# Windowed attention of a hybrid layer: one plan over 64 head groups in pinned order, 129-column value products, gates projected last

## The chip, the cores and the metric

The kernel runs on one core of one Trainium2 chip. The metric is the device time of one execution in microseconds (us); less is better. The engines of the core are named PE (TensorE: matmuls and transposes; PEld is its weight load), DVE (VectorE), ACT (ScalarE), POOL (GpSimd) and SP (SyncE, which here only issues DMAs). Each takes its own instructions in order and waits at semaphores for the others.

## The reference, cut to what matters

A latent stream x of 2048 tokens by 1024 and 256 context tokens go through two layers and a last norm. The even layer mixes by a Fourier transform and by latent attention (8 heads); the odd layer is the one that changes. Its last part per block of 128 tokens is:

```python
h = rmsnorm(x, norm_g[1]) * (1 + scale) + shift
q, k, v, g = split(h @ o_w_in, (1024, 256, 256, 1024))      # rotary on q and k; k, v for the context too
for kv in range(4):                                         # 4 heads of 64 share one k and v
    s = q[block, 4 * kv : 4 * kv + 4] @ k[context + own and both neighbouring blocks].T / 8   # |i - j| <= 128
    m = max(s, sink);  p = exp(s - m)
    o[block, kv] = p @ v / (p.sum() + exp(sink - m))
x = rmsnorm(x + gate * ((o * silu(g)) @ o_w_out), final_g)
```

All of it is float32. The kernel makes float32 products from 2 or 3 matmuls of rounded halves: a value is split into a high part (a cast) and a low part (value minus cast).

## The kernel before, in words

The odd layer starts with its projection. The 18 pieces of 128 tokens (2 of them context) are worked in three sets, and each set goes through five column blocks, one pass each: 0 and 1 are q, 2 is k and v, 3 and 4 are gates. `TP['p2o']` is the order of the columns in the last set; in the other sets it is 0 to 4. So before the change the last five passes are gate, gate, q, q, k with v. Passes write q, k, v (high and low parts) and silu(g) to DRAM (`store_t`, `g1d`), from where the attention loads them. `e6` is a list of work for the attention that is done between the matmuls of the last four passes: constants, keys and values of the first tiles (`prep_k`), q of block 0 (`load_q6`), row maxima of block 0 (`max_all`: four `max_band` and two `max_ctx` for a head group), its `chain`, and the first `aug`.

The attention runs over 16 blocks of 128 tokens, in each over 4 key-value heads, in each over 5 key tiles of 128 (2 of context, 3 of the band; 4 in blocks 0 and 15). One head group is one (block, kv) with its 4 heads: 64 of them, 312 steps (`step6`). A step makes scores for 128 keys by 4 heads x 128 queries in one PSUM bank: a bfloat16 mask matmul (L1813, outer tiles only), L1814 and L1815. The rows appended to the second operand (`Q2`, rows 64 and up) carry the negative maximum, split in halves and picked by a mask: `aug` transposes it (L1566) and multiplies it into place (L1567). ACT then takes the exponential twice, into float32 `pf` (L1819) and float16 `ph` (L1820), and POOL, for some steps DVE, makes the low part `pl` (L1821). The products with v are queued (`pvq`) and done 4 steps later (`lag`): for each of 4 heads L1831 (high by high with the column of ones: 65 columns), L1832 (high by low, 64 columns, into the same 64 columns) and L1833 (low by high, 65). After the last tile of a group DVE makes the quotient (L1837, L1838, L1840) and POOL multiplies it into the gates (L1842).

The maxima of block b + 1 are made during block b: PE makes the scores once more (L1525 for the band, L1538 for the context), DVE reduces them (L1529, L1541), and at 0.94 of the block one `chain` of six DVE operations (L1549 to L1556), one addition and one exponential (L1562) serves all 16 heads. Also in block b + 1 the output of block b is finished: two `out_tr` (4 transposes each, L1868, and a split), 16 `out_mm` of 3 matmuls (`mm3`, L186 to L188), then `out_fin` (square, power, the scaling L1894, the store).

All this stands in one `plan` per block: `at(place, function)` with the place as a share of the block's steps; after each step the plan's functions that are due are called. PE's, DVE's, ACT's and POOL's instructions go to a scheduler, which may change their order; SP's DMAs keep the order in which they are called. The weights of the output projection are loaded and split (`wload`, `wsplit`) in blocks 0 and 1.

## Time and profile before

| | |
|---|---|
| median of 3 runs | 3035.95 us (3033.46 to 3040.3) |
| profiled execution | 3034.24 us, its span 3032.2 us, mean granted TensorE clock 0.983 |
| busy share of the span | PE 94%, POOL 54%, DVE 48%, ACT 47% |
| first score of blocks 0, 1, 2, 14, 15 | 2335.02, 2377.05, 2420.61, 2935.42, 2976.23 us |

The span is the time from the first to the last instruction that the profiler saw; the execution is some 2 us longer. A row of the windows gives a stretch and its length, the busy time of each engine with the number of its instructions in brackets, the mean granted clock of TensorE as a share of full speed (PEclk), the busy share of the DMA engines and GB/s. A row of a timeline gives start and length of an instruction, its engine and line, what it writes and reads, how many of the same kind follow each other (x), and in square brackets how long the engine stood idle before it and what ended that. PE's matmuls are pipelined: rows of neighbours overlap, and the distance of two starts is what one costs. A row of the waits says which line waited for which. A group of instructions has busy us and the mean ns of one, then idle time before it and what ended most of that.

### The profile page before, as it was taken

The numbers are of one execution on the slowest core, as the hardware profiler recorded it, in microseconds if no ns is written. First come the engines' busy times: TensorE is split into PE (matmuls) and PEld (weight loads), VectorE is DVE, ScalarE is ACT, GpSimd is POOL, SyncE is SP. The second block draws the span as 40 slices with busy tenths as digits, with TensorE's granted clock in tenths as the row PEclk, the third lists the DMA queues.
The fourth block names the chain that finished last, engine by engine and source line by source line (L and its number), as shares of the span: only waits on it lengthen the run. The fifth ranks groups of instructions, "written<-read, shape, count | busy, mean of one in ns | idle before, by whom it ended". The sixth has DMA issues, their size and how long they took to land. (4 is left out here: it accounts for less than half of the span.)

```text
span 3032.2 us, 54284 instructions
## 1 busy us (share of the span) xinstructions
PE 2861.0 (94%) x21388; PEld 2299.7 (76%) x21388; DVE 1462.6 (48%) x2884; ACT 1427.4 (47%) x2131; POOL 1632.0 (54%) x1221
## 2 busy tenths in 40 slices
PE   7999999999999999999999998999997899999998
PEld 4787777877777777777777888989786666677666
DVE  3323315453656665666542234323234666676664
ACT  4333213223577777777773332232222645554554
POOL 2202204035588888888784434353443766766665
PEclk9999999999999999999999998999998999999999
DMA  6453335466310111011016545544464333223321
GB/s 240 153 177 134 130 122 173 142 213 223 104 44 26 44 40 44 26 44 40 26 35 232 188 153 177 187 141 162 152 189 156 105 105 98 84 77 93 102 83 45
DMA packets 299399, 357.13 MB, mean 118 GB/s; under 512 B 40884, under 2 KB 210172, under 8 KB 299144
## 3 DMA queue, kind: packets, MB, share of 16 engines
q1 hardware_dynamic: 231320, 258.73, 27.0%
q10 hardware_dynamic: 67824, 94.93, 8.9%
q8 instruction: 168, 2.75, 0.4%
q14 instruction: 87, 0.71, 0.1%
HBM read 245.82 MB, written 107.76 MB: 117 GB/s over the span
## 5 line engine op out<-in xcount | busy, mean ns | idle before, releaser
L186 PE MATMUL psb<-sbr 128*128 128x512 f32 (+3 forms) x2054 | 744.3, 363 | 14.4 <-ACT sbf L1022 5.7
L188 PE MATMUL psb<-sbr 128*128 128x512 f32 (+3 forms) x2054 | 722.9, 352 | 4.8 <-DVE sbr L183 4.8
L187 PE MATMUL psb<-sbr 128*128 128x512 f32 (+3 forms) x2054 | 723.8, 352 | 2.2 <-POOL sbr L183 2.2
L1188 POOL TENSOR_TENSOR sbf<-sbf 128x1024 f16<-128x1024 f32 (+1 forms) x296 | 624.2, 2112 | 140.8 <-ACT sbf L1187 76.9
L155 PE MATMUL psb<-sbr 100*128 100x512 f32 (+1 forms) x2408 | 624.2, 399 | 21.0 <-DVE sbr L955 14.4
L155 PEld LDWEIGHTS psb<-sbr 100*128 100x128 f32 (+1 forms) x2408 | 425.0, 190 | 112.8 <-issue 17.3
L942 DVE TENSOR_REDUCE sbf<-psb 128x1 f32<-128x512 f32 (+1 forms) x584 | 400.7, 690 | 218.1 <-PE psb L155 203.5
L186 PEld LDWEIGHTS psb<-sbr 128*128 128x128 f32 (+1 forms) x2054 | 390.7, 190 | 81.0 <-issue 12.3
L188 PEld LDWEIGHTS psb<-sbr 128*128 128x128 f32 (+1 forms) x2054 | 390.2, 190 | 63.9 <-DVE sbr L183 6.8
L187 PEld LDWEIGHTS psb<-sbr 128*128 128x128 f32 (+1 forms) x2054 | 390.8, 190 | 53.2 <-POOL sbr L183 3.9
L1821 POOL TENSOR_TENSOR sbf<-sbf 128x512 f16<-128x512 f32 x282 | 338.0, 1213 | 116.0 <-issue 60.1
L1186 ACT ACTIVATE sbf<-psb 128x1024 f32<-128x1024 f32 (+1 forms) x296 | 299.6, 1012 | 200.4 <-PE psb L155 180.5
L183 DVE TENSOR_TENSOR sbr<-sbf,sbr 128x512 fp32r<-128x512 f32 (+3 forms) x212 | 209.1, 1014 | 382.2 <-ACT sbr L180 381.1
L180 ACT CAST sbr<-sbf 128x512 fp32r<-128x512 f32 (+4 forms) x286 | 198.2, 731 | 394.5 <-PE psb L187 149.5
L183 POOL TENSOR_TENSOR sbr<-sbf,sbr 128x512 fp32r<-128x512 f32 (+4 forms) x113 | 166.1, 1482 | 367.9 <-ACT sbr L180 226.3
L1819 ACT ACTIVATE sbf<-psb 128x512 f32<-128x512 f32 x312 | 188.4, 604 | 282.1 <-PE psb L1815 249.8
L1187 ACT ACTIVATE sbf<-psb 128x1024 f16<-128x1024 f32 (+1 forms) x296 | 297.8, 1006 | 0.0
L155 PEld LDWEIGHTS <-sbf 128*128 128x128 f16 x4672 | 213.5, 97 | 72.9 <-issue 65.9
L155 PE MATMUL psb<-sbf 128*128 128x129 f16 (+1 forms) x4672 | 256.8, 207 | 5.2 <-DVE sbf L1214 2.9
L1529 DVE CUSTOM_DVE_ANT_0 sbf<-psb,sbf 128x384 bf16<-128x384 f32 (+1 forms) x256 | 137.8, 538 | 119.4 <-PE psb L1525 108.1
L1820 ACT ACTIVATE sbf<-psb 128x512 f16<-128x512 f32 x312 | 188.2, 603 | 5.5 <-DMA vd<-sbf 5.5
L1831 PEld LDWEIGHTS <-sbf 128*128 128x128 f16 x1248 | 115.5, 97 | 68.3 <-issue 61.8
(259 smaller groups left out, 4303.9 us busy)
## 6 DMA issues: line engine op xcount, KB each, us to landing
sbf<-in_o_w_in_t SPq DMA_DIRECT2D x60, 512.0 KB
sbf<-in_w_in_t SPq DMA_DIRECT2D x54, 512.0 KB
sbf<-in_x SPq DMA_DIRECT2D x32, 512.0 KB
sbf<-in_w_mod SPq DMA_DIRECT2D x32, 512.0 KB
sbr<-q1h SPq DMA_DIRECT2D x128, 128.0 KB
h1d<-sbf ACTq DMA_DIRECT2D x9, 1024.0 KB
sbf<-h1d SPq DMA_DIRECT2D x18, 512.0 KB
x1d<-sbf ACTq DMA_DIRECT2D x16, 512.0 KB
```

What stands on the lines that cost most here:

```text
L155: tc.keep_in_program_order(nc.tensor.matmul(*args, **kw))
L180: act.copy(hi, src)
L183: e_lo.tensor_sub(lo, src, hi)
L186: pe.matmul(ps, sh, mh, start=start, stop=False)
L187: pe.matmul(ps, sh, ml, start=False, stop=False)
L188: pe.matmul(ps, sl, mh, start=False, stop=stop)
L942: dve.reduce_max(st["mx"][:, js[0] : js[-1] + 1, c], ps[:, 0 : len(js) * kn].rearrange("p (j k) -> p j k", k=kn), axis=AX.X)
L1186: act.activation(pf[:, :, 0:n], ps[:, :, 0:n], AF.Exp, scale=MLA_SCALE)
L1187: act.activation(ph[:, :, 0:n], ps[:, :, 0:n], AF.Exp, scale=MLA_SCALE)
L1188: pool.tensor_sub(pl[:, :, 0:n], pf[:, :, 0:n], ph[:, :, 0:n])
L1819: act.activation(pf, ps, AF.Exp, scale=GQA_SCALE)
L1821: (dve if (TP["b0"].get("sub", TP["sub"]) if b == 0 else TP["sub"])[kv][n] else pool).tensor_sub(pl, pf, ph)
```

## The change

The order of columns in the last projection set becomes 0, 1, 2, 3, 4. `e6` holds the maxima, chain and aug of two head groups of block 0 where it held all four. The stores of gates wait one turn (`pend`) behind the other work of their pass.

In the attention, PE's instructions are no longer the scheduler's: `pe = pe_ordered` keeps them in the order of the calls. The 16 plans become one, in steps over all 312: for a group that starts at step s, q is asked for at the start of the group five before, the maxima at s - 9 to s - 4.9, the chain at s - 4.9, aug at s - 2.2. The chain is now per group: one DVE reduction over band, context and sink, one ACT copy that scales by -1, one POOL addition, one ACT exponential. The appended rows are 4 instead of 8. `out_tr` and `out_mm` come later in the next block (8.2, 10.2 and from 12.2 steps on, each 0.95 step), so that half of them reach into the block after; block 14 and the end are tighter.

Steps go in pairs. The float32, high and low tiles of a pair are one tile each, POOL subtracts both steps at once (128x1024), and value products are done two steps at a time, at least 6 steps late. A value product is now 129 columns (high by high with the ones, and high by low beside it) and 65 columns (low by high); their order alternates so that a burst ends with 129. The output of a group therefore takes two PSUM banks, and there is one such tile where there were two of one bank; DVE adds the second half with four operations per group. The final scaling of a block goes from DVE to an ACT copy, a POOL product and an ACT product.

The diff, cut to its core:

```diff
-    'p2o': [3, 4, 0, 1, 2],
+    'p2o': [0, 1, 2, 3, 4],
...
+    def chain(b, kv):
+        m = sm6.tile([P, 4], F32, tag="m", name=f"m6_{b}_{kv}")
+        dve.reduce_max(m, C6["mx", 4 * (b % 2) + kv], axis=AX.X)
+        v = VM[b, kv] = sm6.tile([P, 4], F32, tag="vm", name=f"vm6_{b}_{kv}", bufs=3)
+        act.activation(v.bitcast(F32R), m, AF.Copy, bias=SHIFT / GQA_SCALE, scale=-1.0)
+        es = ES[b, kv] = sm6.tile([P, 4], F32, tag="es", name=f"es6_{b}_{kv}", bufs=4)
+        pool.tensor_add(es, v, C6["sk8"][:, 4 * kv : 4 * kv + 4])
+
+    def sink(b, kv):
+        act.activation(ES[b, kv], ES[b, kv], AF.Exp, scale=GQA_SCALE)
...
     def aug(b, kv):
...
+        pe.transpose(ps[0:4, 0:P], VM[b, kv], ident)
...
+            Q2[b, kv][64:68, :].rearrange("p (j t) -> p j t", t=P),
+            ps[0:4, None, 0:P].to_broadcast([4, 4, P]), C6["mask4"],
...
     e6 = [
...
+        [const6, nop, *pk[0], nop, *pk[1], nop, *pk[2], nop, *pk[3]],
+        [nop] * 4 + [lambda: load_q6(0, 0)] + [nop] * 4,
+        [nop] * 4 + max_all(0) + [lambda: chain(0, 0)],
+        [lambda: load_q6(0, 1), lambda: load_q6(0, 2), *pk[4]] + [nop] * 4 + max_all(1) + [lambda: chain(0, 1), nop]
+        + [lambda: aug(0, 0)],
     ]
...
+    pe = pe_ordered
+    pps, ppv, ppo = psum(3), psum(1), psum(1)
...
+    def step6(b, kv, n, t, nk, x):
...
+        if not x:
+            PF["f"] = pp6.tile([P, 2, 512], F32, tag="pf", name=f"pf6_{b}_{kv}_{t}", bufs=2)
+            PF["h"] = pp6.tile([P, 2, 512], F16, tag="ph", name=f"ph6_{b}_{kv}_{t}")
+            PF["l"] = pp6.tile([P, 2, 512], F16, tag="pl", name=f"pl6_{b}_{kv}_{t}")
+        pf, ph, pl = PF["f"], PF["h"][:, x], PF["l"][:, x]
+        act.activation(pf[:, x], ps, AF.Exp, scale=GQA_SCALE)
         act.activation(ph, ps, AF.Exp, scale=GQA_SCALE)
...
+        if b == 15 and kv == 3 and n > 1:
+            (pool if x else dve).tensor_sub(pl, pf[:, x], ph)
+        elif x:
+            pool.tensor_sub(PF["l"], pf, PF["h"])
...
         def pv():
...
+                O[b, kv] = ppv.tile([P, 1024], F32, tag="o", name=f"o6_{b}_{kv}")
...
+                o = O[b, kv][:, j * 256 : j * 256 + 129]
...
+                if j % 2 and n:
+                    pe.matmul(o[:, 0:65], pl[:, js], v[:, kv, 0:65], start=False, stop=False)
+                    pe.matmul(o, ph[:, js], v[:, kv, 0:129], start=False, stop=last)
+                else:
+                    pe.matmul(o, ph[:, js], v[:, kv, 0:129], start=n == 0 and j % 2 == 0, stop=False)
+                    pe.matmul(o[:, 0:65], pl[:, js], v[:, kv, 0:65], start=False, stop=last and j % 2 == 1)
...
+                dve.tensor_add(den, p4[:, :, 64:65], ES[b, kv][:, :, None])
...
                 dve.tensor_mul(t1, p4[:, :, 0:64], den.to_broadcast([P, 4, 64]))
+                for j in range(4):
+                    dve.scalar_tensor_tensor(t1[:, j], p4[:, j, 65:129], den[:, j], t1[:, j], op0=ALU.mult, op1=ALU.add)
...
+                pool.tensor_mul(g, g, t1)
+        pvq.append((pv, n == nk - 1))
...
         v = sm6.tile([P, 1], F32, tag="v", name=f"v6s_{b}")
         y = sm6.tile([P, 1], F32, tag="y", name=f"y6s_{b}")
-        dve.tensor_scalar(v, ss, 1.0 / D, EPS, op0=ALU.mult, op1=ALU.add)
+        act.activation(v, ss, AF.Copy, bias=EPS, scale=1.0 / D)
         rsqrt(y, v)
-        dve.scalar_tensor_tensor(x, x, y, C6["fgb"], op0=ALU.mult, op1=ALU.mult)
+        pool.tensor_mul(x, x, C6["fgb"])
+        act.mul(x, x, y)
         sp.dma_start(out[b * P : (b + 1) * P, :], x)
...
+    nts = [len(tiles_of(b)) for b in range(16)]
+    S = [4 * sum(nts[:b]) for b in range(17)]
+    groups = [(b, kv) for b in range(16) for kv in range(4)]
+    start = [S[b] + kv * nts[b] for b, kv in groups]
+    plan = []
...
+    at(-1, lambda: (sink(0, 0), sink(0, 1)))
+    for u, (b, kv) in enumerate(groups):
+        if u > 2:
+            at(start[u - 5] + 0.3 if u > 5 else -1, lambda b=b, kv=kv: load_q6(b, kv))
+        if u > 1:
+            s0 = start[u] - 9
+            for j in range(4):
+                at(s0 + 0.8 * j, lambda b=b, kv=kv, j=j: max_band(b, kv, j))
+            for jj in range(2):
+                at(s0 + 3.2 + 0.8 * jj, lambda b=b, kv=kv, jj=jj: max_ctx(b, kv, jj))
+            at(s0 + 4.1, lambda b=b, kv=kv: (chain(b, kv), sink(b, kv)))
+        if u:
+            at(start[u] - 2.2, lambda b=b, kv=kv: aug(b, kv))
+    for x in range(TP["wa"], 17):
+        w0 = 1.5 * (x - TP["wa"] - 1) if x > TP["wa"] else -1
+        if x < 16:
+            at(w0, lambda x=x: wload(*wl_[x]))
+        if x > TP["wa"]:
+            at(w0 + 1.6, lambda x=x: wsplit(*wl_[x - 1]))
+    at(S[1] + 1, out_const)
+    for b in range(16):
+        at(S[b] - 0.5, lambda b=b: g_load(b))
+        if b < 13:
+            at(S[b] + 6.6, lambda b=b: [f() for f in prep_k(b + 5)])
         if b == 15:
+            break
+        s1 = S[b + 1]
+        t0, t1, m0, md = (8.2, 10.2, 12.2, 0.95) if b < 13 else (8.2, 10.2, 12.2, 0.45) if b == 13 else (3, 6, 6.5, 0.42)
+        at(s1 + t0, lambda b=b: out_tr(b, 0))
+        at(s1 + t1, lambda b=b: out_tr(b, 1))
+        at(s1 + m0, lambda b=b: out_load(b))
+        for i in range(16):
+            at(s1 + m0 + md * i, lambda b=b, i=i: out_mm(b, i // 8, i % 8))
+        at(s1 + m0 + md * 16 + 0.6, lambda b=b: out_fin(b))
+    at(S[15] + 14, lambda: out_load(15))
+    at(S[15] + 13.4, lambda: tail_tr(0, 0, 4))
+    for i in range(8):
+        at(S[15] + 15 + 0.1 * i, lambda i=i: tail_mm(i // 2, i % 2))
+    plan.sort(key=lambda z: z[:2])
+
+    def run(pos):
+        while plan and plan[0][0] < pos:
+            plan.pop(0)[2]()
+
+    def run_pv(keep):
+        while len(pvq) > keep:
+            pvq.pop(0)[0]()
+
+    run(0)
+    g = late = 0
+    for b in range(16):
         for kv in range(4):
+            for n, t in enumerate(tiles_of(b)):
+                turn = g % 2 == 0 and len(pvq) > 5 and pvq[0][1]
+                if turn:
+                    pvq.pop(0)[0]()
+                    late = 1
+                step6(b, kv, n, t, nts[b], g % 2)
+                g += 1
+                run(min(g - 0.5, S[15] + 14.9))
+                if g % 2 == 0:
+                    run_pv((6 if b < 15 else 4) + late)
+                    late = 0
+                    run(min(g, S[15] + 14.9))
+    tail_tr(1, 4, 2)
+    run(S[15] + 15.45)
+    run_pv(2)
+    run(S[16])
+    tail_mm(4, 0)
+    run_pv(0)
+    tail_mm(4, 1)
+    tail_mm(5, 0)
+    tail_mm(5, 1)
+    tail_tr(2, 6, 2)
```

Three places show how the order of instructions moves. In the rows, sbf, sby, sbr and psb are SBUF and PSUM areas.

On PE, in the middle of the attention, the change over from one burst of value products to the next in the kernel before:

```order
L1833 MATMUL psb<-sbf 128x65
L1814 MATMUL psb<-sbr 128x512
L1815 MATMUL psb<-sbr 128x512
L186 MATMUL psb<-sbr,sby 128x512
L187 MATMUL psb<-sbr,sby 128x512
L188 MATMUL psb<-sbr,sby 128x512
L1525 MATMUL psb<-sbr 128x384
```

And in the changed kernel between the last product of one group and the first of the next (in attention L124 is every matmul and L128 every transpose, x3 is three alike):

```order
L124 MATMUL psb<-sbf 128x129
L124 MATMUL psb<-sbr,sby 128x512 x3
L124 MATMUL psb<-sbr 128x512 x2
L124 MATMUL psb<-sbr 128x384
L124 MATMUL psb<-sbr,sby 128x512 x3
L124 LDWEIGHTS sbf
L124 MATMUL psb<-sbf 128x512
L124 MATMUL psb<-sbr 128x512 x2
L124 MATMUL psb<-sbr 128x384
L124 LDWEIGHTS sbf
L124 MATMUL psb<-sbf 128x129
```

A burst is followed by the scores of two steps where it was one, with the output projection and row maxima among them: 13 matmuls stand between the two bursts.

On SP, the store of a finished block (out) and the loads of q behind it, before:

```order
L150 DMA out<-sbf 128x1024
L150 DMA sbf<-g1d_16009 128x1024
L150 DMA sbf<-x1d_5169 128x1024
L150 DMA sbr<-q1h_15990 64x4x128
L150 DMA sbr<-q1l_15998 64x4x128
L150 DMA sbr<-q1h_15990 64x4x128 x2
```

And in the changed kernel:

```order
L119 DMA sbr<-kTl_16033 64x4x128
L119 DMA sbf<-vd_16048 128x520
L119 DMA out<-sbf 128x1024
L119 DMA sbr<-q1h_15990 64x4x128
L119 DMA sbr<-q1l_15998 64x4x128
L119 DMA sbr<-q1h_15990 64x4x128
L119 DMA sbf<-x1d_5169 128x1024
```

The store moves from the head of a block to a place behind the loads of keys and values; the q load that follows it serves a group five later, where it was the next block's first group.

On ACT, the instructions about the end of a block's output, before (L1889 is the square, L1562 the sink exponential of all 16 heads):

```order
L1889 ACTIVATE sbf<-sbf 128x1024
L1819 ACTIVATE sbf<-psb 128x512
L1820 ACTIVATE sbf<-psb 128x512
L1562 ACTIVATE sbf<-sbf 128x16
L1819 ACTIVATE sbf<-psb 128x512
```

And in the changed kernel (L1787 and L1788 are a step's exponentials, L1520 the scaling of a maximum, L1525 the sink exponential of a group, L1869 and L1872 the new scalings, L149 a split):

```order
L1520 ACTIVATE sbf<-sbf 128x4
L1525 ACTIVATE sbf<-sbf 128x4
L1787 ACTIVATE sbf<-psb 128x512
L1788 ACTIVATE sbf<-psb 128x512
L1787 ACTIVATE sbf<-psb 128x512
L1788 ACTIVATE sbf<-psb 128x512
L1866 ACTIVATE sbf<-sbf 128x1024
L1787 ACTIVATE sbf<-psb 128x512
L1788 ACTIVATE sbf<-psb 128x512
L1869 ACTIVATE sbf<-sbf 128x1
L149 CAST sby<-psb 128x512
L1872 ACTIVATE sbf<-sbf 128x1024
```

Between the square and the last scaling stands one step's pair of exponentials, and a sink exponential stands right behind the scaling whose result POOL adds for it.

## Rows read from the trace of the kernel before

**Rows 1.** Windows of blocks 0, 1, 2-13, 14, 15: busy times, granted clock
```profile
2335.02:2377.05 42.03, 27.87 (x214) 19.17 (x213) 19.41 (x48) 23.44 (x45) 30.76 (x29) 0.72 0.43 133
2377.05:2420.61 43.56, 39.83 (x388) 30.17 (x386) 30.96 (x82) 24.08 (x48) 29.83 (x29) 1.00 0.40 110
2420.61:2935.42 514.81, 476.32 (x4567) 357.05 (x4563) 342.57 (x829) 277.52 (x541) 336.80 (x312) 0.99 0.31 89
2935.42:2976.23 40.81, 38.53 (x387) 29.09 (x383) 26.61 (x70) 23.12 (x46) 28.07 (x26) 1.00 0.25 79
2976.23:3032.20 55.97, 44.77 (x397) 32.87 (x393) 18.98 (x40) 23.27 (x46) 31.58 (x29) 0.96 0.16 57
```

**Rows 2.** Windows of two slices at the end of the projection; columns as before
```profile
2290.00:2300.00 10.00, 6.46 (x39) 6.46 (x40) 7.10 (x16) 3.22 (x6) 2.65 (x3) 0.66 0.26 86
2310.00:2320.00 10.00, 8.08 (x45) 8.11 (x46) 3.84 (x12) 0.62 (x1) 2.70 (x3) 0.66 0.53 159
```

**Rows 3.** Timeline of PE at two waits: start us, us, instruction [idle before]
```profile
2293.54 0.58 PE L1525 MATMUL psb<-sbr 128*128 128x256 f32 x1 [7.43 <-DVE sbf L1529]
...
2349.61 0.98 PE L1525 MATMUL psb<-sbr 128*128 128x384 f32 x2 [6.25 <-DMA sbr<-q1l]
```

**Rows 4.** Waits in blocks 2 to 13: us in total, times, longest us
```profile
PE psb L1525 <- DMA sbr<-q1l: 14.2, 8, 2.2
PE psb L1566 <- DVE sbf L1555: 9.0, 12, 0.8
PE psb L1868 <- DVE sby L183: 8.0, 12, 0.7
```

**Rows 5.** Chain that ended last, one step of it: start us, us, what
```profile
2561.36 5.00 DMA sbr<-q1l
```

**Rows 6.** Timeline of PE, one burst and what follows: start us, us
```profile
2702.38 0.20 PE L1831 MATMUL psb<-sbf 128*128 128x65 f16 x1
...
2702.76 0.48 PE L1814 MATMUL psb<-sbr 128*128 128x512 f32 x1
2703.08 0.40 PE L1815 MATMUL psb<-sbr 72*128 72x512 f32 x1
2703.31 0.40 PE L1538 MATMUL psb<-sbr 128*128 128x256 f32 x2
```

**Rows 7.** Timeline of ACT, a table load in block 0
```profile
2342.67 1.28 ACT L1562 ACT_TABLE_LOAD   x1 [2.52 <-DMA kTl<-sbf]
```

**Rows 8.** Timeline of PE in the latent attention
```profile
922.98 0.87 PE L155 MATMUL psb<-sbf 128*128 128x129 f16 x16
923.65 2.10 PE L155 MATMUL psb<-sbr 100*128 100x512 f32 x8
```

**Rows 9.** Window of the latent attention; columns as in rows 1
```profile
900.00:1500.00 600.00, 584.43 (x5313) 462.38 (x5312) 371.28 (x715) 438.60 (x479) 496.33 (x249) 1.00 0.13 38
```

**Rows 10.** Groups of instructions, blocks 2 to 13: busy us, mean ns
```profile
L1821 POOL TENSOR_TENSOR sbf<-sbf 128x512 f16<-128x512 f32 x216 | 259.0, 1214 | 83.0 <-issue 43.1 <-ACT sbf L1820 26.1 <-POOL sbf L1821 10.2
L1821 DVE TENSOR_TENSOR sbf<-sbf 128x512 f16<-128x512 f32 x24 | 28.0, 1168 | 9.2 <-ACT sbf L1820 8.3 <-POOL sbf L1883 0.9
L1894 DVE SCALAR_TENSOR_TENSOR sbf<-sbf 128x1024 f32<-128x1024 f32 x12 | 26.1, 2177 | 18.9 <-POOL sbf L191 18.9
L1840 DVE TENSOR_TENSOR sbf<-psb,sbf 128x256 f32<-128x256 f32 x49 | 20.8, 424 | 1.7
L1838 DVE RECIPROCAL sbf<-sbf 128x4 f32<-128x4 f32 x48 | 8.4, 175 | 0.8
L1837 DVE TENSOR_TENSOR sbf<-psb,sbf 128x4 f32<-128x4 f32 x48 | 7.7, 160 | 1.8
```

**Rows 11.** Groups of the whole run, POOL and ACT: 128x1024 forms
```profile
L1188 POOL TENSOR_TENSOR sbf<-sbf 128x1024 f16<-128x1024 f32 (+1 forms) x296 | 624.2, 2112 | 140.8 <-ACT sbf L1187 76.9 <-PE psb L155 47.9 <-PE psb L159 9.2
L1355 ACT ACTIVATE sbf<-sbf 128x1024 f32<-128x1024 f32 x18 | 20.3, 1148 | 17.2 <-POOL sbf L191 9.8 <-DMA x1d<-sbf 7.3
```

**Rows 12.** Group of the whole run, VectorE: half-sum additions of the latent attention
```profile
L1214 DVE SCALAR_TENSOR_TENSOR sbf<-psb,sbf 128x64 f32<-128x64 f32 x144 | 31.0, 275 | 0.0
```

More of the change, by code (lines that the diff above doesn't have):

```diff
@@ L1458, in const6 @@
         dve.tensor_scalar(sk8, sk8, 1.0 / GQA_SCALE, None, op0=ALU.mult)
+        for u in range(8):
+            C6["mx", u] = c6.tile([P, 4, 3], F32, name=f"mx6{u}")
+            act.copy(C6["mx", u][:, :, 2], sk8[:, u % 4 * 4 : u % 4 * 4 + 4])
         C6["kkc"] = c6.tile([P, 4, NCTX], F32R, name="kkc")
@@ L1519, in max_band @@
         m0 = 0 if b else P
-        if b not in MX:
-            MX[b] = sm6.tile([P, 2, 16], F32, tag="mx", name=f"mx6_{b}")
-        mx = MX[b]
+        mx = C6["mx", 4 * (b % 2) + kv]
         s = lo % RING
@@ L1587, in tile_hybrid @@
     e6 = [
-        [const6, nop, *pk[0], nop, *pk[1], nop, *pk[2]],
-        [*pk[3], nop, *pk[4]],
-        [lambda: load_q6(0, 0)] + [nop] * 5 + max_all(0),
-        [lambda kv=kv: load_q6(0, kv) for kv in range(1, 4)] + [nop] * 3 + max_all(1) + max_all(2) + max_all(3)
-        + [lambda: chain(0)] + [nop] * 3 + [lambda: aug(0, 0)],
+        [const6, nop, *pk[0], nop, *pk[1], nop, *pk[2], nop, *pk[3]],
[3 more added lines that the diff above has]
+        + [lambda: aug(0, 0)],
     ]
@@ L1826, in pv @@
             if n == 0:
-                O[b, kv] = ppv.tile([P, 512], F32, tag="o", name=f"o6_{b}_{kv}")
+                O[b, kv] = ppv.tile([P, 1024], F32, tag="o", name=f"o6_{b}_{kv}")
             for j in range(4):
-                o = O[b, kv][:, j * P : j * P + 65]
+                o = O[b, kv][:, j * 256 : j * 256 + 129]
                 js = slice(j * P, (j + 1) * P)
-                pe.matmul(o, ph[:, js], v[:, kv, 0:65], start=n == 0 and j == 0, stop=False)
-                pe.matmul(o[:, 0:64], ph[:, js], v[:, kv, 65:129], start=False, stop=False)
-                pe.matmul(o, pl[:, js], v[:, kv, 0:65], start=False, stop=last and j == 3)
+                if j % 2 and n:
[4 more added lines that the diff above has]
+                    pe.matmul(o[:, 0:65], pl[:, js], v[:, kv, 0:65], start=False, stop=last and j % 2 == 1)
             if last:
@@ L1869, in out_tr @@
         ks = slice(4 * q, 4 * q + 4)
-        split(yh[:, ks, :], yl[:, ks, :], ps.rearrange("p (k t) -> p k t", k=4), act if TP["e_yh"] else dve, dve)
+        split(yh[:, ks, :], yl[:, ks, :], ps.rearrange("p (k t) -> p k t", k=4), act, dve)
     def out_mm(b, hf, k):
@@ L1900, in tail_tr @@
     def tail_tr(q, k0, n):
+        if not q:
+            YT[15] = (
+                yp6.tile([P, KT, P], F32R, tag="yh", name="yh6_15"),
+                yp6.tile([P, KT, P], F32R, tag="yl", name="yl6_15"),
+            )
         yh, yl = YT[15]
@@ L1914, in tail_mm @@
         mm3(ZP[hf], yh[:, k, :], yl[:, k, :], wh, wl, k == 0, k == KT - 1)
-    def tail_x(_):
-        tail_tr(1, 4, 2)
-        for i in range(2):
-            if pvq:
-                pvq.pop(0)()
-            tail_mm(4, i)
-        while pvq:
-            pvq.pop(0)()
-        tail_mm(5, 0)
-        tail_tr(2, 6, 2)
-        tail_mm(5, 1)
     def tail_end():
@@ L1952, in tail_end, with tiles_of, at @@
             (sp if hf else act).dma_start(out[15 * P : 16 * P, hsl], x[:, hsl])
-    parity = 0
-    for b in range(16 - TP["nb"], 16):
+    def tiles_of(b):
+        lo, hi = band(b)
+        return [0, 1] + [2 + i for i in range(lo, hi + 1)]
+    nts = [len(tiles_of(b)) for b in range(16)]
[3 more added lines that the diff above has]
+    plan = []
+    def at(pos, f):
+        plan.append((pos, len(plan), f))
@@ L1956, in tile_hybrid, with g_load @@
+    def g_load(b):
         G[b] = yp6.tile([P, D], F32, tag="g", name=f"g6_{b}", bufs=2)
         sp.dma_start(G[b], g1d[b])
[L1958 to L1978 removed]
@@ L2013, in tile_hybrid @@
-        plan.sort(key=lambda z: z[:2])
-        lo, hi = band(b)
-        tiles = [0, 1] + [2 + i for i in range(lo, hi + 1)]
-        if len(tiles) == 5:
-            tiles = [tiles[x] for x in T["ord"]]
-        tot = 4 * len(tiles)
-        done = 0
-        for kv in range(4):
-            for n, t in enumerate(tiles):
-                step6(b, kv, n, t, len(tiles))
-                done += 1
-                if b == 0 and done == 1:
-                    sink(0)
-                parity ^= 1
-                while plan and plan[0][0] < done / tot:
-                    plan.pop(0)[2]()
-                if parity == 0 or TP["grp"] == 1:
-                    while len(pvq) > (TP["lag"] if b < 15 else TP["zlag"]):
-                        pvq.pop(0)()
```

155 lines of the change are left out of this document (21 added, 134 removed).

## The prediction

> **What bounds the kernel now.** The change touches the odd layer from the last projection passes on, some 740 of 3032 us, so I read that stretch by stages first: the table of windows cut at the first score of blocks 0, 1, 2, 14 and 15 [rows 1]. TensorE (PE) is busy 476.3 of 514.8 us in blocks 2 to 13: a block takes 514.81 / 12 = 42.9 us, 39.7 of them PE's. VectorE (342.6), GpSimd (POOL, 336.8) and ScalarE (ACT, 277.5) are at 28.5, 28.1 and 23.1 us a block. So PE sets the interior, and only two things shorten it: less PE work, or fewer of its 3.2 idle us. Block 0 is another case: PE busy 27.9 of 42.0 at a granted clock of 0.72, POOL 30.8. Block 1 carries a block's full PE work, 39.8 of 43.6.
>
> Then the end of the projection. The slices 2290 to 2300 and 2310 to 2320 stand at a granted clock of 0.66 with PE 6.5 and 8.1 us busy [rows 2]: a mean between the two levels (1.2 and 2.4 GHz), after stretches in which PE stood. The timeline of PE shows why it stood [rows 3]: 7.43 us ahead of 2293.54, when the next matmul was a row maximum (L1525) whose PSUM buffer VectorE had not read, and 6.25 us in block 0 for the load of q. Nothing dense stood behind those maxima, because the last two passes are q columns with maxima packed between them.
>
> Of the idle time in blocks 2 to 13 the view of waits names 14.2 us for q's low half, 9.0 for the chain of row maxima (L1555), 8.0 for the split of the transposed output (L183) [rows 4]: 2.6 us a block. The chain of work that ended last leads through such a load: issued at 2561.36, it takes 5.00 us to land [rows 5], and on SyncE (SP), whose queue is in order, it stands behind an output store that waits for the last step of the block before.
>
> **The change, part by part.** *The maxima and the order of projection.* Gates last means that the maxima of two head groups only (12 operations, not 24) stand before block 0, with dense gate matmuls among them. Taken back: the 7.4 us stand; one of the two slow slices, 10 x 0.34 = 3.4 (the other's loss overlaps the stand); 12 maxima of about 0.23 [rows 6], 2.8, which go into block 0 where PE has room. Against it: a gate's PSUM buffer also waits for ACT, bounded by 0 and the 7.4 it replaces; ACT has little to do there, so I take 1.1. Block 0 starts 12.5 us earlier (bounds 6 and 14). ACT's function changes forth and back twice in the gate passes, four table loads at 1.28 us [rows 7], 5.1 us of ACT alone; they hide as long as ACT's queue runs ahead of the six PSUM buffers, and cost up to 5.1 if not.
>
> *Block 0.* q, k and v are in SBUF earlier, so the 6.25 us stand goes; POOL's work does not: about 31 us [rows 1] of subtractions, weight splits and gate products, in larger pieces. I take POOL's 31 plus 3 us of start: 34, minus 8.0.
>
> *Value products.* Before, 12 matmuls a step take from 2702.38 to 2702.76, 0.38 us; the first f32 matmul behind them then takes 0.32, the next 0.23 [rows 6]. The new form, 129 and 65 columns, is already in the kernel: the latent attention's 16 such matmuls take 922.98 to 923.65, 0.67 us, 0.335 for 8 [rows 8]. Twenty steps save 20 x 0.045 = 0.9 us a block. In pairs, ten changes from f16 to f32 go: 10 x 0.09 = 0.9. PE work is 39.7 - 1.8 = 37.9 us a block (39.7 if neither form nor pairing helps; 37.0 if the ten changes that stay, now behind a 129-column matmul, cost nothing either).
>
> *PE's idle time.* q is asked for five groups ahead and no more behind the store in its own block's load; the chain is per group and 2.7 steps ahead of its transpose; the transposes come 8.2 and 10.2 steps into the next block, when the gate products are long done, and 2.7 steps lie between a group's chain and its transpose. The 2.6 us named go. SP issues as many transfers as before: the key and value loads move to 6.6 steps into a block, for a block five later, and the g load to half a step ahead of its block; both have several us more than the 5.00 that a q load took. The gates that are now written last belong to blocks 12 to 15, so no g load of block 0 waits for them. What comes instead is not in the trace: PE's order is now fixed, so a wait holds everything behind it. The nearest row is the latent attention, also in fixed order with the same burst: PE 584.43 of 600 busy, 97.4% [rows 9]. 37.9 / 0.974 = 38.9 us a block, 4.0 less, times 12 is 48.0 (bounds: 36.5 a block, 76.8; 42.0, 10.8).
>
> *What moves to VectorE, ACT and POOL.* A block's 18 subtractions of 1.214 us on POOL and two of 1.168 on VectorE become ten of the 128x1024 form, 2.112 us by the latent attention [rows 10, 11]: POOL 21.9 to 21.1. The final scaling leaves VectorE (2.18) for POOL (one 128x1024 product, about 2.1) and ACT (1.15, L1355). With small chain operations POOL comes to about 30.2 us a block, ACT to 25.7, VectorE to 27.5 (four additions per group of 0.275 [rows 12] against the six chain operations and the subtractions that leave). All stand below 38.9, so I cost them at nothing; the cover is PE's own time, and POOL is the one to lose it: at 36.5 a block it would be 83% busy.
>
> *Block 1, 14, 15.* The output projection starts 12.2 steps into the next block, so block 1 keeps 9 of its 16 parts: 7 x 3 x 0.23 = 4.8 less, and the interior's 4.0: minus 8.8. Block 14 catches up, plus 4.8 - 4.0: plus 0.8. Block 15 keeps its parts; at 44.8 of 56.0 PE-busy [rows 1], its end is a sequence from the last group to the store that only loses two small turns: minus 1.0 (bounds -4 and +4).
>
> **Sum.** 12.5 + 8.0 + 8.8 + 48.0 - 0.8 + 1.0 = 77.5 us. The profiled execution took 3034.24 us (span 3032.2): 2956.7. The median of the runs shown is 1.7 above it, so I say 2958 us.
>
> **The rivals.** *A, slower: one output buffer.* Before, two PSUM tiles O alternate between groups. After, there is one, two banks wide, and the next group's first product must wait until VectorE has read the last: den 0.160, reciprocal 0.175, product 0.424 [rows 10], and four additions of 0.275 [rows 12], 1.86 us. Sixty-four groups make 119 us if nothing covers it: 2958 + 119 = 3077. It decides from 77.5 / 64 = 1.2 us a group on. The Trainium skill, "Perfetto Trace Analysis", section Matmuls under Optimizing Tensor Performance, speaks for this rival: independent groups should rotate through PSUM banks so that reading one overlaps with the next one's matmuls; by that rule this change gives up its overlap. No run before shows a single buffer in this place. Against it, from the order after: 13 matmuls of the next pair of steps stand between a group's last product and the next one's first, 13 x 0.23 = 3.0 us, more than 1.86. It needs VectorE to be late by over a microsecond in every group, with row maxima ahead of it in VectorE's queue that is possible at times, not always. Chance 0.07.
>
> *B: ACT held behind POOL.* ACT runs in order, and now holds instructions that wait for POOL: the sink exponential of each group, behind the small addition that stands after a 2.1 us subtraction, and the final scaling, behind POOL's 128x1024 product and a power. Before, one such exponential per block. Up to 3 x 2.1 us a block, on top of 25.7: ACT still has room on the average, but only three score buffers, about 1.9 us each, lie between it and PE. If one wait in a block goes through, with 2.5 us: 2958 + 12 x 2.5 = 2988. Chance 0.22.
>
> *C: the waits only move.* Fixed order turns each early or late operand into a PE stand, and the interior stays at 42.0; with the start and blocks 0 and 1 alone: 77.5 - 48.0 + 10.8 = 40.3, and about ten lost for the same reason in block 0, it ends 30.3 below the profiled execution, with the 1.7 at 3006. Chance 0.10. That the change doesn't do what it says is in this case too: a shorter burst brings nothing if PE then waits for POOL's subtraction ahead of it.
>
> *D: better.* PE at 36.5 us a block, because there is more to win than the busy time shows: its rows overlap (0.40 us long, 0.23 apart, [rows 6]), so that up to 0.17 us of standing at each of a block's 20 bursts counts as busy. Two thirds of that, 2.4 us, gone with the bursts' number and the fixed order: 2958 - 12 x 2.4 = 2929. Chance 0.17.
>
> **How the numbers follow.** The forecast has 0.44.  The range reaches from below D, 2918 (D with blocks 0 and 1 four us shorter each, the start's bound of 14 and nothing lost in block 14: 2929 - 8 - 1.5 - 0.8 = 2918.7), to just short of C, 3003; it leaves out A, the greater half of C and the outer end of D, less than 2 in 10. A measurement of this kernel can tell about 0.2%, 6 us. Slower is A and the worst of C: 0.08; within 0.2%: 0.02; faster: 0.90.
>
> **What would show it.** After the change: first score of block 0 near 2322; blocks 2 to 13 at 38.9 us with PE over 97% busy; no PE wait on q loads; the last two passes at a granted clock near 1. Rival A shows as PE waiting on the four additions at each group's first product; B as ACT waiting on POOL in the rows of the sink exponential or the scaling, with PE waiting on the exponentials; C as PE waits on POOL's subtraction or on VectorE's row maxima. I am wrong if the interior blocks stay above 41.5 or fall below 36.5.

## The result, and the profile after

The changed kernel takes 3055.69 us (median of 4 runs, 3050.65 to 3059.44) against 3035.43 of the kernel before: a ratio of 1.0063, 95% interval 1.0042 to 1.0084. It is 20 us slower where 77 less were forecast. The profiled execution took 3050.65 us, its span 3048.8.

The windows of the changed kernel, cut at the first exponential (L1787) of blocks 0, 1, 2, 14 and 15; columns as in [rows 1]:

```profile
2340.90:2372.80 31.90, 22.16 (x149) 16.85 (x149) 16.99 (x54) 22.14 (x50) 25.97 (x20) 0.83 0.59 179
2372.80:2411.00 38.20, 35.99 (x286) 28.26 (x286) 26.97 (x83) 22.88 (x52) 29.30 (x22) 0.87 0.44 129
2411.00:2923.10 512.10, 470.04 (x3602) 370.17 (x3602) 308.38 (x961) 300.49 (x648) 361.95 (x265) 0.94 0.30 89
2923.10:2974.10 51.00, 46.06 (x335) 36.33 (x334) 28.08 (x95) 26.70 (x59) 32.76 (x26) 0.93 0.15 48
2974.10:3048.80 74.70, 50.80 (x323) 38.58 (x322) 24.16 (x69) 25.55 (x53) 32.78 (x26) 0.81 0.10 36
```

Blocks 2 to 13 take 42.7 us each, as before, but with a granted clock of 0.94, not 0.99. Block 14 takes 51.0 and the rest 74.7. Cut at the first exponential in both kernels (in the kernel before the exponentials of blocks 0 and 1 come 9.1 and 7.3 us behind the first score of [rows 1], so the cuts differ there), and with the even layer's last row scaling as the start, since the part ahead of it is the same and takes 1816 to 1827 us in the profiled executions:

| us | before | forecast | changed | product behind the cast (n1) | fastest (n2) |
|---|---|---|---|---|---|
| last scaling to block 2 | 595.9 | 566.6 | 595.0 | 596.4 | 580.6 |
| blocks 2 to 13, each | 42.9 | 38.9 | 42.7 | 37.5 | 37.5 |
| block 14 | 40.8 | 41.6 | 51.0 | 45.1 | 44.9 |
| block 15 and the end | 54.6 | 53.6 | 74.7 | 71.4 | 60.4 |

The forecast's column is the one before plus the terms of the sum (12.5 + 8.0 + 8.8 = 29.3 in the first row). Against this column the changed kernel is longer by 28 us up to block 2, 45 in blocks 2 to 13, 9 in block 14 and 21 behind it.

Where a block's time goes: one stretch of ACT, POOL and PE in an interior block of the changed kernel, from the timeline of all engines:

```profile
2724.46 1.06 ACT L1866 ACTIVATE sbf<-sbf 128x1024 bf16<-128x1024 f32 x1
...
2726.57 0.58 ACT L149 CAST sby<-psb 128x512 fp32r<-128x512 f32 x1
2726.66 2.38 POOL L1871 TENSOR_TENSOR sbf<-sbf 128x1024 f32<-128x1024 f32 x1
...
2728.99 0.55 POOL L160 TENSOR_TENSOR sbf<-sbf 128x1 f32<-128x1 f32 x1
...
2729.57 1.15 ACT L1872 ACTIVATE sbf<-sbf 128x1024 f32<-128x1024 f32 x1 [2.42 <-POOL sbf L160]
...
2730.63 0.58 ACT L1787 ACTIVATE sbf<-psb 128x512 f32<-128x512 f32 x1
...
2731.11 0.59 ACT L1788 ACTIVATE sbf<-psb 128x512 f16<-128x512 f32 x1
...
2731.74 0.38 PE L124 MATMUL psb<-sbf 128*128 128x512 bf16 x1 [1.96 <-ACT sbf L1788]
...
2732.54 0.61 ACT L149 CAST sby<-psb 128x512 fp32r<-128x512 f32 x1
...
2733.18 0.69 DVE L152 TENSOR_TENSOR sby<-psb,sby 128x512 fp32r<-128x512 f32 x1 [2.58 <-ACT sby L149]
...
2733.92 1.33 PE L124 MATMUL psb<-sbr,sby 128*128 128x512 f32 x3 [1.34 <-DVE sby L152]
```

ACT makes the square (L1866) and the first cast of the transposed output, and then comes to the final scaling (L1872), whose factor POOL has not made: product 2.38 and power 0.55. It stands 2.42 us, and behind it in its queue stand the exponentials and the second cast. PE's next score has no free buffer until an exponential has read one, and PE stands 1.96 us, and 1.34 more for the split of that cast. The granted clock of the stretches that follow (last three columns: clock, DMA share, GB/s):

```profile
2730.00:2731.50 1.50, 0.00 (x0) 0.00 (x0) 0.60 (x4) 1.50 (x3) 0.00 (x0) 1.00 0.00 0
...
2734.50:2736.00 1.50, 1.50 (x5) 1.13 (x5) 0.00 (x0) 1.18 (x3) 1.50 (x3) 0.50 0.81 229
2736.00:2737.50 1.50, 1.50 (x6) 1.11 (x5) 1.00 (x3) 1.08 (x2) 0.98 (x2) 0.50 0.39 158
2737.50:2739.00 1.50, 1.50 (x28) 1.22 (x27) 0.81 (x3) 0.00 (x0) 1.50 (x1) 0.92 0.00 0
```

After the two stands of this block PE works some 3 us at 0.50, the lower level. The mean of 0.94 over the 512.1 us amounts to 5.1 us a block at that level. The waits of blocks 2 to 13 show that the stands come once in every block (times: 12), where [rows 4] had the three waits that are gone; for PE, these two are all that the view has:

```profile
ACT sbf L1525 <- POOL sbf L1522: 71.8, 48, 2.2
...
ACT sbf L1872 <- POOL sbf L160: 29.2, 12, 2.5
...
PE psb L124 <- ACT sbf L1788: 23.7, 12, 2.0
...
PE psb L124 <- DVE sby L152: 16.1, 12, 1.3
```

The end of the projection has a new stand, some 12 us with its small pieces, ahead of the place where [rows 3] had the one of 7.43 us; of that one, 4.07 us ahead of 2301.81 are left. PE, changed kernel, in the k and v pass:

```profile
2240.95 0.39 PE L155 MATMUL psb<-sbr 128*128 128x256 f32 x1 [2.93 <-ACT sbr L149]
...
2247.85 0.58 PE L155 MATMUL psb<-sbr 128*128 128x256 f32 x1 [3.71 <-ACT sbr L149]
...
2252.67 0.58 PE L155 MATMUL psb<-sbr 128*128 128x256 f32 x1 [3.51 <-ACT sbr L149]
```

L149 is here the cast of this pass's weights. On SP their loads (in_o_w_in) stand between constants and key loads of the attention:

```profile
2229.92 4.19 SPq L119 DMA_DIRECT2D sbf<-in_c_bandT  x2
2235.19 0.38 SPq L119 DMA_DIRECT2D sbf<-in_o_w_in_t  x1
2235.66 1.42 SPq L119 DMA_DIRECT2D sbr<-kTh  x2
...
2240.26 0.39 SPq L119 DMA_DIRECT2D sbf<-in_o_w_in_t  x1
2241.53 2.52 SPq L119 DMA_DIRECT2D sbr<-kTh  x2
```

By the view of waits ACT's casts (L149) between 2225 and 2260 wait for these constants and weights, and for the stores of q (q1l, q1h) that ACT issues itself:

```profile
ACT sbr L149 <- DMA sbf<-in_c_bandT: 8.8, 1, 8.8
...
ACT sbr L149 <- DMA q1l<-sbf: 5.5, 2, 4.2
ACT sbr L149 <- DMA sbf<-in_o_w_in_t: 3.8, 1, 3.8
ACT sbr L149 <- DMA q1h<-sbf: 1.8, 1, 1.8
```

And the end, from the timeline of all engines:

```profile
3015.19 1.06 ACT L1866 ACTIVATE sbf<-sbf 128x1024 bf16<-128x1024 f32 x1 [1.88 <-POOL sbf L1860]
...
3017.43 1.87 DVE L1790 TENSOR_TENSOR sbf<-sbf 128x512 f16<-128x512 f32 x1 [3.40 <-ACT sbf L1788]
...
3019.23 0.15 DVE L1811 TENSOR_TENSOR sbf<-psb,sbf 128x4 f32<-128x4 f32 x1
...
3019.75 1.15 ACT L1872 ACTIVATE sbf<-sbf 128x1024 f32<-128x1024 f32 x1 [1.86 <-POOL sbf L160]
...
3021.46 1.15 POOL L1790 TENSOR_TENSOR sbf<-sbf 128x512 f16<-128x512 f32 x1 [1.74 <-ACT sbf L1788]
3022.57 0.72 POOL L1818 TENSOR_TENSOR sbf<-sbf 128x256 f32<-128x256 f32 x1
...
3023.34 0.69 PE L128 MATMUL psb<-sbf 128*128 128x128 f32 x2 [8.10 <-POOL sbf L1818]
```

PE stands 8.10 us ahead of two transposes that are fixed ahead of the other work of the end; they need POOL's gate product (L1818), and this the quotient (L1811). The quotient stands on VectorE behind a subtraction (L1790) which waits for ACT's exponential, held up by block 14's square (L1866), for which ACT stood 1.88 us. The gate product stands on POOL behind a second subtraction (L1790), whose exponential stood behind block 14's scaling (L1872).

### The profile page after: what moved, and what is told of

Its sections match the earlier page's. It is cut to its first block, busy times and chain, and to the rows that moved or that the text cites. A ratio compares the mean times of both kernels' runs of the same rounds, so it can differ in the third digit from the quotient of the medians.

```text
span 3048.8 us, 52019 instructions
## 1 busy us (share of the span) xinstructions
PE 2862.3 (94%) x20140; PEld 2321.2 (76%) x20140; DVE 1420.4 (47%) x3064; ACT 1465.1 (48%) x2285; POOL 1664.6 (55%) x1159
## 5 line engine op out<-in xcount | busy, mean ns | idle before, releaser
L124 PE MATMUL psb<-sbr 96*128 96x512 f32 (+6 forms) x3492 | 948.8, 401 | 30.0 <-DVE sbr L924 14.4
L124 PEld LDWEIGHTS psb<-sbr 96*128 96x128 f32 (+3 forms) x3492 | 629.9, 194 | 196.0 <-issue 48.1
L124 PE MATMUL psb<-sbf 128*128 128x129 f16 (+2 forms) x7288 | 443.6, 212 | 38.0 <-ACT sbf L1788 29.8
L124 PEld LDWEIGHTS <-sbf 128*128 128x128 f16 (+1 forms) x7288 | 345.1, 99 | 121.8 <-issue 107.1
L1792 POOL TENSOR_TENSOR sbf<-sbf 128x1024 f16<-128x1024 f32 x155 | 331.6, 2140 | 185.2 <-ACT sbf L1788 136.0
L149 ACT CAST sbr<-sbf 128x512 fp32r<-128x512 f32 (+4 forms) x286 | 198.7, 732 | 402.3 <-PE psb L156 155.1
L124 PE MATMUL psb<-sbr,sby 128*128 128x512 f32 (+1 forms) x740 | 245.1, 438 | 18.8 <-DVE sby L152 18.2
L1787 ACT ACTIVATE sbf<-psb 128x512 f32<-128x512 f32 x312 | 186.3, 597 | 134.8 <-PE psb L124 133.2
L1788 ACT ACTIVATE sbf<-psb 128x512 f16<-128x512 f32 x312 | 187.0, 599 | 0.1
```

What stands on the lines that cost most here:

```text
L124: tc.keep_in_program_order(nc.tensor.matmul(*args, **kw))
L1787: act.activation(pf[:, x], ps, AF.Exp, scale=GQA_SCALE)
L1788: act.activation(ph, ps, AF.Exp, scale=GQA_SCALE)
L1792: pool.tensor_sub(PF["l"], pf, PF["h"])
```

## The experiments

Theory S: one stand of ACT per block, at the final scaling in its queue, costs what PE won. Its rivals were K (the sink exponentials, which stand 72 us for POOL), F (the fixed order of PE), POOL's load as such, and A of the prediction. All but one run make the full computation. Each batch ran beside the kernel before; the difference to its median there is given. These medians lie between 3034.49 and 3037.18, so that differences between batches, to the changed kernel above all, are uncertain by some 3 us.

**e1_fin_dve.** The scaling back on VectorE:

```diff
-        act.activation(v, ss, AF.Copy, bias=EPS, scale=1.0 / D)
+        dve.tensor_scalar(v, ss, 1.0 / D, EPS, op0=ALU.mult, op1=ALU.add)
         rsqrt(y, v)
-        pool.tensor_mul(x, x, C6["fgb"])
-        act.mul(x, x, y)
+        dve.scalar_tensor_tensor(x, x, y, C6["fgb"], op0=ALU.mult, op1=ALU.mult)
```

> The changed kernel with the final scaling of a block back on VectorE (one scalar and one 128x1024 operation) in place of ACT copy, POOL product and ACT product; all else as changed. Theory S (one stand per block): in the changed kernel ACT stands 2.4 us a block at its last scaling, waiting for POOL's 128x1024 product and the power behind it; the exponentials behind it come late, PE stands some 3.3 us and then runs some 3 us at a granted clock of 0.5. Without it blocks 2 to 13 go from 42.7 to about 38 us and the whole to about 2995 (from 3053). Rival K (the sink exponentials, which stand 72 us in all for POOL in these blocks, set ACT's pace): the blocks stay above 42. Rival F (the fixed order of PE is what costs): they stay above 41.5, and other waits take its place.

3004.07 us, 31 below before (ratio 0.9901, 0.9881 to 0.9921), 52 below the changed kernel. The interior in its windows, and all of PE's waits there:

```profile
2420.00:2884.40 464.40, 442.30 (x3591) 349.68 (x3602) 319.77 (x985) 287.60 (x625) 338.17 (x253) 1.00 0.33 98
```
```profile
PE psb L128 <- DVE sby L152: 16.2, 12, 1.4
PE psb L124 <- DVE sby L152: 5.9, 12, 0.5
```

38.7 us a block at a clock of 1.00: S holds. K falls, and so does F as the cause of the blocks' length. The 1.8 us a block that PE still stands are for the split that VectorE makes: in the block at 2707, the scaling, which waited 0.98 us for POOL's power, stands right ahead of a split, and PE waits 1.35 us for that.

**e2_mul_late.** The same operations on the same engines, ACT's product (and the store) called 5 steps later. This run leaves out block 14's scaling and store, and its products read x after the next block's load.

```diff
-        act.mul(x, x, y)
+        FIN[b] = x, y
...
+        at(s1 + m0 + md * 16 + 5.6, lambda b=b: out_fin2(b))
```

> The changed kernel with the same operations of the final scaling on the same engines, but ACT's last product and the store called 5 steps later, so that POOL is done when ACT comes to it. It tells a wait in ACT's queue from the work itself. Theory S: as the run with VectorE, blocks 2 to 13 at about 38 us, the whole at about 2995, ACT's wait for the power gone. If instead POOL's extra 2.4 us a block is what costs (POOL as the pace), this run stays near 3050 while the one with VectorE gains. Rivals K and F: both stay above 3035.

2988.61 us, 47 below before (0.9847, 0.9824 to 0.9870); blocks 2 to 13 at 37.4. POOL's work is as in the changed kernel, so its load is not the cost. What was left out made it worth a second try.

**e3_pe_free.** The line `pe = pe_ordered` ahead of the attention taken out.

> The changed kernel with PE's order in the attention left to the scheduler again, all else as changed. Rival F (fixed order turns late operands into PE stands): blocks 2 to 13 below 40 us, the whole below 3000. Theory S: the scheduler orders by its own estimate and can't step around a wait on the chip either, so the stand at ACT's last scaling stays; blocks 2 to 13 between 41.5 and 44, the whole between 3035 and 3070.

3017.16 us, 18 below before (0.9942, 0.9924 to 0.9961), between what the two theories said. Blocks 2 to 13 take 41.2, with ACT's 29.3 us of waiting for the power as in the changed kernel. Of PE's two waits there the first is left (its lines have other numbers in this run):

```profile
PE psb L1778 <- ACT sbf L1787: 23.8, 12, 2.0
```

So S holds for the first stand, and F for the second: the 16.1 us of waiting for the split are gone, and with them 1.5 us a block, 17 in all. The end falls from 74.7 to 60: the fixed order costs 15 us in block 15 and after.

**e4_p2o_back.** The order of passes [3, 4, 0, 1, 2], and `e6` as before with the maxima of two groups only.

> The changed kernel with the old order of the last projection passes (gates, q, q, k and v) and the work between them placed as before, though still with the maxima of two head groups only. Theory W (in the new order the weights of the k and v pass come late behind constants, key loads and the q stores, and PE stands some 12 us at 2238 to 2256 in place of the old 10.7 at the maxima): the whole within 5 us of the changed kernel, the stand at 2240 gone and one of 3 to 10 us back at the maxima. Rival (gates last is worth the 12.5 us of the forecast even so): 8 to 13 us slower than the changed kernel.

3043.13 us, 8 above before (1.0030, 1.0017 to 1.0042), 12.6 below the changed kernel, which is more than was expected: from the last scaling to the first exponential 508.8 us against 524.9 (before: 518.0). The stand near 2240 is gone. At the maxima 1.55 and 3.06 us are left for VectorE, and two waits of 0.9 for q. But block 0 takes 36.0 us, against 31.9: PE stands there for exponentials that ACT makes late, and ACT's row names a store of k:

```profile
2340.47 0.60 ACT L1787 ACTIVATE sbf<-psb 128x512 f32<-128x512 f32 x1 [3.76 <-DMA kTl<-sbf]
...
2343.43 0.59 PE L124 MATMUL psb<-sbf 128*128 128x512 bf16 x1 [12.80 <-ACT sbf L1788]
```

**m1_mul_late.** e2 with nothing left out: x is loaded 5 steps later, the product called 3.6 to 5 steps later (in block 14, whose output is finished at the end, hardly later).

> The changed kernel with ACT's last product of a block called 3.6 to 5 steps later, and the load of x for the next block 5 steps later so that its buffer is free; the full computation, all else as changed. Theory S: ACT finds POOL done or nearly so, blocks 2 to 13 at 37.4 to 38.5 us, the whole at 2985 to 2995. If the gain of the earlier run came from the missing store of one block and not from the wait, it stays above 3030.

3033.36 us, as before (1.0001, 0.9989 to 1.0013). Blocks 2 to 13 take 41.0. The product has come to lie ahead of the second cast (L149), and the waits say what that does:

```profile
PE psb L124 <- DVE sby L152: 30.1, 12, 2.5
...
ACT sbf L1878 <- POOL sbf L160: 17.6, 12, 1.5
```

The exponentials are in time now, but the cast behind the product is not, and PE stands 2.5 us for its split. So S needed sharpening: what counts is what stands behind the waiting product in ACT's queue. The clock's mean is 0.96 here.

**m2_pv_old.** m1 with the value products of before (12 matmuls, two output tiles of one bank, no additions on VectorE).

> The run above with the value products of the kernel before: 12 matmuls a step of 65, 64 and 65 columns into one bank, two output tiles in turn, no additions by VectorE; pairs, fixed order and plan as changed. By the forecast's term the 129-column form is worth 0.9 us a block here (the pairs stay): blocks 2 to 13 about 0.9 longer than the run above, the whole 11 to 15 longer. Rival A (the single output tile costs a wait per group): shorter than the run above, by up to 1.8 us a group, and 5 to 50 us in all.

3034.09 us (0.9997, 0.9985 to 1.0009), equal to m1. Its interior is 499.7 us against 492.2, 0.63 a block more for the old form, and its end 66.3 against 73.5. The two cancel. The run changes the form, the tiles and the additions together: in the end PE's stand ahead of the two transposes is 5.58 us where m1 has 8.10, and the wait for the additions (0.76) is gone.

**m3_sink_late.** m1 with the sink exponential 4 steps behind its chain.

> The run with the late product, and the sink exponential of each group called 4 steps later than its chain, so that POOL has made its sum when ACT comes to it. Theory S: ACT's 72 us of standing for POOL's small addition in blocks 2 to 13 lie in ACT's slack; the blocks stay within 0.3 us of the run above and the whole within 5 us. Rival K: the blocks lose 0.5 us or more, the whole 6 or more.

3036.01 us (1.0008, 0.9997 to 1.0018), the blocks at 41.1 as m1. That speaks against K, but weakly: ACT still stands 47.4 us for the sinks in these blocks, where m1 has 65.2.

**m4_best.** m1 with e4's order of passes, and `pe = nc.tensor` from block 15 on.

> The run with the late product, the old order of the projection passes, and PE's order left to the scheduler from block 15 on. From the earlier runs: the order is worth 12 us (3055.7 to 3043.1), the free order of PE in the end 13 (72 to 60 us from block 15's first exponential to the end): the whole at 2965 to 2975. If the end's loss comes from the order of operations on VectorE and POOL and not on PE, the last part stays at 70 us and the whole near 2978.

3010.28 us (0.9926, 0.9911 to 0.9941). The expectation rested on e2's interior, which m1 did not have; against m1 it gains 23, where its two terms, 12 and 13, make 25.

**n1_split_first.** The changed kernel with one order more, on ACT; the product and the store are called 3 to 6 steps later for it (in block 14 hardly later, and without the order). Cut to the order:

```diff
-        act.mul(x, x, y)
+        with tc.issue_after(HI[b + 1, 1].ins):     # the second cast of the next block's output
+            act.mul(x, x, y)
```

> The changed kernel with ACT's last product of a block issued behind the second cast of the transposed output of the next block (an order on ACT alone); the full computation, all else as changed. The first run with a late product was 65 us below the changed kernel, but it left out the store of one block and read x after the next block's load, and the second one, where the product came ahead of that cast, gained only 22: PE waited 2.5 us a block for the split. Theory S, made sharper (what counts is what stands behind the waiting product in ACT's queue): blocks 2 to 13 at 37.4 to 38 us, the whole at 2985 to 2995. If the 65 us came from the missing work, blocks 2 to 13 stay at 41 and the whole near 3033.

2987.56 us, 50 below before (0.9837, 0.9822 to 0.9852) and 68 below the changed kernel. The interior, and PE's and ACT's waits in it:

```profile
2416.40:2865.90 449.50, 443.66 (x3579) 350.04 (x3602) 308.24 (x961) 293.72 (x648) 360.95 (x265) 1.00 0.33 101
```
```profile
ACT sbf L1525 <- POOL sbf L1522: 103.8, 48, 3.0
...
PE psb L124 <- DVE sby L1849: 3.6, 12, 0.3
```

37.5 us a block, PE busy 98.7% at a clock of 1.00; the 0.3 us a block for the split are all that PE waits. S holds, with the full computation. ACT stands even longer for the sinks, at no cost, which decides against K.

**n3_const_late.** The changed kernel with constants and key loads in the k and v pass.

> The changed kernel with the new order of the projection passes, but the attention's constants and key loads moved one pass later, behind the weights of the k and v pass in SP's queue. If it is these loads that hold the weights up (SP's queue), PE's stand of 12 us near 2240 goes and the whole is 8 to 14 us below the changed kernel. If it is ACT, whose queue holds the casts of the weights behind the issues of the q stores, the stand stays and the whole is within 4 us of the changed kernel.

3053.91 us (1.0056, 1.0041 to 1.0071), as the changed kernel. The stand neither went nor stayed: 2.5 us are left near 2245, and 11.49 came ahead of 2295.09, in the next pass, with the loads. Neither expectation names this.

**n4_tail.** n1 with the transposes of heads 8 to 11 (`tail_tr(1, 4, 2)`) called behind the output products that don't need them.

> The run with the product behind the cast, with the transposes of heads 8 to 11 of block 15 called behind the output products that don't need them; order of PE fixed. PE stood 6.6 to 8.1 us ahead of these transposes in the runs before, for POOL's product, and ran at a granted clock near 0.5 behind it. Expected: that stand gone or under 1 us, the whole 6 to 10 us below the run with the product behind the cast. If POOL's product is late because VectorE and ACT are late (the last group's exponentials behind the final scaling of block 14), PE stands at the next place and the gain is under 4 us.

2977.32 us (0.9800, 0.9784 to 0.9816), 10 below n1. The stand of 8.1 us, which n1 has too, is gone; 65.3 us for block 15 and the end, 6.1 less. A wait of 1.88 us for the additions (L1816) is new.

**n2_best.** n4's place of the transposes, PE free from block 15 on, e4's order of passes, on n1.

> The run with the product behind the cast, with the old order of the projection passes, PE's order free from block 15 on, and the transposes of heads 8 to 11 of block 15 called behind the output products that don't need them. By the earlier runs 12 us from the order, 9 from the free order in the end, 0 to 6 from the transposes: 2960 to 2972. If the gains don't add, near 2985.

2962.59 us, 75 below before (0.9756, 0.9741 to 0.9772): the fastest.

**p1_const_early.** The changed kernel with constants and key loads in the first q pass, behind a gate pass.

> The changed kernel with the new order of the projection passes, but the attention's constants and key loads one pass earlier than in it, in the first q pass, right behind the gate passes of the set before. The old order took PE's stand of 12 us near 2240 away, one pass later moved it on. If the stand needs both, the loads in SP's queue between the weights and the stores of q or k on ACT in the pass before, it goes: from the last norm to the first exponential about 508 us instead of 524, the whole 10 to 16 below the changed kernel, 3040 to 3046. If the loads alone make it, it moves to the first q pass and the whole stays within 4 us of the changed kernel.

3048.26 us (1.0047, 1.0026 to 1.0068), 7 below the changed kernel; 512.3 us to the first exponential. The stand is down to some 3.5 us in small pieces; 3.0 and 5.1 us stay at the gates' first weights and at a maximum. So the long stands came with both, the loads in SP's queue and the q or k stores on ACT ahead of them. Where the loads come behind gates, PE stands 3.5 us in this pass (p1) or not at all (e4); where the weights come behind q stores without the loads, 2.5 us (n3). No run was made to part the two.

**p2_best_gates.** n2 with the new order of passes and p1's loads.

> The fastest version so far (product behind the cast, PE free from block 15 on, late transposes; 2962.6 with the old order of passes) with the new order of passes and the loads one pass earlier. If gates last is worth what the forecast said once its weights are in time (12.5 us ahead of block 0 against the kernel before; the old order with 12 maxima gave 9 to 11), it is at 2955 to 2965. If the stand stays, near 2978.

2968.95 us (0.9796, 0.9773 to 0.9820), 6 above n2: gates last is no gain even with its weights nearly in time.

## Why the prediction was wrong, step by step

- **PE's work and idle time** (39.7 to 37.9 us a block, 38.9 with 97.4% busy): right in kind, and too careful. With the stand away a block takes 37.5 (n1), 37.0 of them busy, between the forecast and rival D. The 129-column products take 0.67 us for 16 here too; the form is worth 0.63 us a block in m2, where 0.9 were put down.
- **What moves to VectorE, ACT and POOL: the step that failed.** "All stand below 38.9, so I cost them at nothing." The shares were sized well (POOL 30.2 a block as forecast, ACT 25.0), but a share is no cover. The final scaling was a wait inside ACT's queue, with the exponentials and a cast behind it. Rival B was this mechanism, with a chance of 0.22 and 2.5 us a block. ACT's wait has that size (2.42), but PE lost twice as much: 42.7 - 37.5 = 5.2, of which PE's two stands are 3.3; the rest goes with the clock of 0.50 behind them. The second stand, for the split, rival B did not have; e3 shows that the fixed order is needed for it. Twelve blocks: 62 us, and block 14 six more. The other half of B, the sink exponentials, costs nothing (n1). The interior stayed above 41.5, by the prediction's own words the sign of being wrong.
- **The order of projection** (12.5 us earlier): by the first exponential the start came 7 later instead, and by the first score, the sign that the prediction gave, 14: at 2338.88, 522.9 us behind the last scaling, against 508.9 before. The wait of PE for its gates, taken at 1.1, was not the one that came: the weights of the pass between were late, and 4.07 of the 7.4 at the maxima stayed. The reading that the last two passes before were q was wrong, too: the last was k and v. e4 divides the term: twelve maxima fewer bring 9.2 us by the first exponential (518.0 to 508.8), gates last loses 16.1; by block 2 it has lost 13.2, because the old order makes block 0 longer.
- **Blocks 0 and 1** were to get 16.8 us shorter together. By the exponentials they get 7.8 shorter (40.2 + 37.7 to 31.9 + 38.2), block 1 at a clock of 0.87. Here the two cuts differ by what ACT was late in the kernel before, so the miss is not divided between start and blocks; the row to block 2 has it whole: 0.9 gained for 29.3.
- **Block 15 and the end** (minus 1.0): plus 20. It was read as a sequence that hardly changes; the fixed order put transposes ahead of work that was ready. n4 wins 6.1 of it by moving them (10 in the medians). With a free order in the end it is at 60.4 in n2, where it was 65.3.
- **Rival A** (one output tile): in the interior PE's waits name no L1816; at the turn to block 15 and in it there is one each (0.80 and 0.96 us in the changed kernel). m2's end is 7 us shorter, more than these two waits explain, and as m2 takes the additions away along with the single tile, it doesn't show which of the two did it. The rule of the Trainium skill ("Perfetto Trace Analysis", Matmuls), that groups should rotate through banks so that reading one overlaps with the next, agrees with the two waits in the end, and not with the interior, where 13 matmuls stand between two groups.

With the stand gone and three more edits of order, n2 is at 2962.6, where 2958 was forecast for the changed kernel. That is no proof of the sum, but in good part luck: one of the edits takes the new order of projection back, and by the rows of the table n2's blocks 2 to 13 are 17 us below the forecast, and the other rows 24 above it. How much of the end's remaining 60 us against 54.6 is the plan and how much the output tile stays open.

## What to carry to other kernels

A small operation moved to an idle engine is not free when it waits there: look at what stands behind it in that engine's queue and who is fed by it, not at the engine's busy share. Where the bound engine then stands, add what it loses at the lower clock afterwards. A fixed order costs next to nothing where every operand has steps to spare (PE waits 0.3 us a block in n1), and costs at the ends, where it doesn't. Whether it beats the scheduler's order in the interior, once the stand is away, wasn't tried.

## What the runs showed of the hardware that was not expected

Stands of 1.96 and 1.34 us close together are followed by some 3 us at a granted clock of 0.50 in the block shown, 5.1 on the mean, and make a block 5.2 us longer. One stand of 2.5 us a block (m1) goes with a mean clock of 0.96; in e1 stands of up to 1.4 and 0.5 us in a block leave the clock at 1.00. POOL's 128x1024 product with a float32 result takes 2.38 us, where the subtraction with a float16 result takes 2.14 of the same size. A power of one column per partition takes 0.55 us on POOL.
